# Staging the output weights of a hybrid decoder layer in seven idle buffers instead of one

## The chip, the cores and the metric

The kernel runs on one core of one Trainium2 chip. The metric is the device time of one execution in microseconds (us); a profile adds, for one execution, when each instruction ran on each engine (PE = TensorE, DVE = VectorE, ACT = ScalarE, POOL = GpSimd, SP = the queue that issues the DMAs).

## The reference, cut to what matters

One decoder layer over 2048 tokens of width 1024: an input projection feeds three head groups, their gated outputs are concatenated, mapped by one output matrix and normalised. The part around the change is the end:

```
cat = concat([o_att * silu(g_att), o_ssm * silu(g_ssm), o_mem * silu(g_mem)])   # (2048, 1024)
sub = cat @ w_out                                                               # (1024, 1024)
h   = layer_norm(DN_ALPHA * x + sub, ln_g, ln_b)
```

`o_att` is sparse attention (8 query heads, the keys of each query chosen by an indexer), `o_ssm` a state-space scan with a GLU, `o_mem` attention into 256 memory tokens.

## The kernel before, in words

Tokens are cut into 16 tiles of 128. In a first phase the input projection is made and the keys are chosen. In the second phase (`phase2`) the attention goes through (tile, head pair) items; tile 15, the longest, comes last. After the twelfth finished tile `stage_s5` runs the state-space group, and directly behind it `open_out` brings in the output weights. After the last attention tile, `out_prep` makes the operands of output tiles 0 and 1, and then `outputs` does all 16 output tiles.

Matmuls in full precision are made from rounded halves: a matrix is split in a high half (rounded copy) and a low half (the rest), and three products are added. So `open_out` makes two copies of `w_out`, `woh` and `wol`. It does so in eight slices of 128 x 1024 (one slice per 128 rows of `w_out`): a DMA brings the slice into a staging tile (L1217), ACT rounds it to `woh` (L1218), POOL subtracts to get `wol` (L1219). The staging tile is named `xh` and has one buffer, so the DMA of a slice waits until POOL is through with the slice before.

`out_prep` for a tile loads `cat` (three DMAs, L1226 to L1228) and the gates `aG` (three DMAs, L1230 to L1232), takes the tanh of the gates into `xh` on ACT (L1234), forms gate times (tanh + 1) on DVE (L1235) and multiplies into `cat` on POOL (L1236). PE transposes `cat` (L1243), ACT rounds to `ch` (L1244), DVE makes `cl` (L1245). For tiles 0 and 1 these tiles lie in the pool of `open_out`, with one buffer each of `xh`, `cat` and `aG` and two each of `ch` and `cl`; every one is 4 KB per partition. For the later tiles they lie in a pool that takes the place of the attention's memory. `out_mm` does 48 matmuls of 512 columns for a tile (L1260 to L1262), adds the residual on DVE (L1263) and normalises.

In the attention, PE makes logits into `pl` (L1116, L1117; two PSUM buffers), DVE adds the mask into `S` (L1118), ACT takes the exponential in place (L1123), PE transposes into `pt` (L1140), ACT rounds to `hi` (L1144), DVE makes `lo` (L1145), PE multiplies with V into `acc` (L1147, L1148). At the end of an item ACT copies `acc` to `oT` (L1153; one buffer), PE transposes (L1156), DVE scales (L1160) and SP stores to `OAD` (L1162).

The code gives a program order; what stands behind what in the queue of an engine is settled when the kernel is compiled, by a simulated timeline (`schedule_with_timeline_sim=True`), with waits put in where data or buffers need them. Each engine then works through its queue in order. The branch behind `fallback` is for inputs on which the key choice failed.

Of the kernel before, what the change touches and what calls it, by code (L numbers as in the profile page):

```python
# [10 lines left out]
F32 = mybir.dt.float32  # L11
F32R = mybir.dt.float32r
# [4 lines left out]
OP = mybir.AluOpType  # L17
# [5 lines left out]
D = 1024  # L23
NT = 16
KT = 8
# [62 lines left out]
class Layer:  # L88
# [1120 lines left out]
    def open_out(self, sp):  # L1209
        nc = self.nc  # L1210
        wo = (sp.tile([128, KT, D], F32R, name="woh"), sp.tile([128, KT, D], F32R, name="wol"))
        gb = sp.tile([128, 2, D], F32, name="gb")
        nc.sync.dma_start(out=gb[:, 0], in_=self.t["ln_g"][None, :].broadcast_to([128, D]))
        nc.sync.dma_start(out=gb[:, 1], in_=self.t["ln_b"][None, :].broadcast_to([128, D]))
        for i in range(KT):
            r = sp.tile([128, D], F32, name="xh", bufs=1)
            nc.sync.dma_start(out=r, in_=self.t["w_out"][:, i * D:(i + 1) * D])  # L1217
            nc.scalar.activation(wo[0][:, i], r, AF.Copy)  # L1218
            nc.gpsimd.tensor_tensor(wo[1][:, i], r, wo[0][:, i].bitcast(F32), op=OP.subtract)  # L1219
        return wo, gb  # L1220

    def out_prep(self, i, sp, nb=1, cb=2):
        nc = self.nc
        g = nc.gpsimd
        cat = sp.tile([128, D], F32, name="cat", bufs=nb)
        nc.sync.dma_start(out=cat[:, 0:512], in_=self.OAD[i])  # L1226
        nc.sync.dma_start(out=cat[:, 512:768], in_=self.OSD[i * 128:(i + 1) * 128])
        nc.sync.dma_start(out=cat[:, 768:1024], in_=self.OMD[i])  # L1228
        G = sp.tile([128, D], F32, name="aG", bufs=nb)
        nc.sync.dma_start(out=G[:, 0:512], in_=self.GAD[i])  # L1230
        nc.sync.dma_start(out=G[:, 512:768], in_=self.GSD[i])
        nc.sync.dma_start(out=G[:, 768:1024], in_=self.GMD[i])  # L1232
        th = sp.tile([128, D], F32, name="xh", tag="xh", bufs=nb)
        nc.scalar.activation(th, G, AF.Tanh, scale=0.5)  # L1234
        nc.vector.scalar_tensor_tensor(G, th, 1.0, G, op0=OP.add, op1=OP.mult)  # L1235
        g.tensor_tensor(cat, cat, G, op=OP.mult)  # L1236
        ch = sp.tile([128, KT, 128], F32R, name="ch", bufs=max(cb, nb))
        cl = sp.tile([128, KT, 128], F32R, name="cl", bufs=max(cb, nb))
        for a in range(2):
            pt = self.ps_a.tile([128, 4, 128], F32, name="pt", bufs=3)  # L1240
            for j in range(4):
                k = 4 * a + j
                nc.tensor.transpose(pt[:, j], cat[:, k * 128:(k + 1) * 128], self.ident)  # L1243
            nc.scalar.activation(ch[:, 4 * a:4 * a + 4], pt, AF.Copy, scale=0.5)  # L1244
            nc.vector.scalar_tensor_tensor(cl[:, 4 * a:4 * a + 4], pt, 0.5, ch[:, 4 * a:4 * a + 4].bitcast(F32),  # L1245
                                           op0=OP.mult, op1=OP.subtract)
        return ch, cl
# [31 lines left out]
    def outputs(self, tiles, wo, gb, sp, nb=1):  # L1279

        for i in tiles:
            if i not in self.cc:
                self.cc[i] = self.out_prep(i, sp, nb, 1)
            self.out_mm(i, self.cc.pop(i), wo, gb, sp, nb)
            for j in range(i + 1, min(i + 1 + AHEAD, NT) if nb > 1 else 0):
                if j not in self.cc:
                    self.cc[j] = self.out_prep(j, sp, nb, 1)

    def flag(self):

# [122 lines left out]
```

## Time and profile before

| | |
|---|---|
| time, median of 3 runs | 1452.05 us (1448.55 to 1458.51) |
| profiled execution, its own time | 1448.58 us |
| span of the profiled execution | 1446.8 us |
| PE busy | 1340.5 us (93%) |
| DVE busy | 1055.4 us (73%) |
| ACT busy | 876.8 us (61%) |
| POOL busy | 521.8 us (36%) |

The span is what the trace covers; 1.8 us of the execution's time lie outside it. Busy time of an engine is the sum over its instructions, and an average over stages that have different limits.

### The profile page before, as it was taken

The page shows a single profiled execution, that of the slowest core. Times are in us where ns is not written, and L with a number is a line of the kernel's source. Part 1 is how long each engine was busy: PE and PEld are TensorE (multiplying, and loading weights), DVE is VectorE, ACT ScalarE, POOL GpSimd, SP SyncE. Part 2 cuts the span into 40 slices and gives each one's busy share as a digit, 9 for nine tenths or more (in the row PEclk, how much of TensorE's full clock was granted, in tenths as well). Part 3 has the DMA queues.
Part 4 walks back from the last instruction along what each step waited for, and adds up shares of the span by engine and source line. Part 5 has one row for each costly group of instructions (what it writes and reads, how often), then busy time and mean ns, then how long its engine had stood idle before and what let it go on. Part 6 is the DMA issues. An engine that isn't in the chain of part 4 may idle for free.

```text
span 1446.8 us, 25157 instructions
## 1 busy us (share of the span) xinstructions
PE 1340.5 (93%) x8398; PEld 1182.1 (82%) x8398; DVE 1055.4 (73%) x2191; ACT 876.8 (61%) x1727; POOL 521.8 (36%) x1028
## 2 busy tenths in 40 slices
PE   7898899998869999999999999999999998699996
PEld 5687789997758988988798999987878987588885
DVE  4545786699676998855778889887887885365763
ACT  4576866775547745356788888876655776222221
POOL 1777544345991110041000000037873003344441
PEclk9899999999979999999999999999999999799999
DMA  9897355456536477742222111032221132565532
GB/s 346 269 314 252 133 176 183 146 186 223 188 95 209 161 240 259 229 147 92 88 66 86 53 47 42 14 104 75 45 58 31 41 113 79 176 203 175 189 102 75
DMA packets 128714, 206.58 MB, mean 143 GB/s; under 512 B 25088, under 2 KB 81792, under 8 KB 128320
## 3 DMA queue, kind: packets, MB, share of 16 engines
q1 hardware_dynamic: 128576, 204.89, 43.4%
q8 instruction: 68, 1.11, 0.3%
q14 instruction: 70, 0.57, 0.1%
HBM read 124.00 MB, written 77.10 MB: 139 GB/s over the span
## 4 chain that ended last, share of the span: by engine, by line
PE 63%; DVE 10%; POOL 9%; DMA 8%; issue 5%; ACT 5%; SPq 1%; POOLq 0%; ACTq 0%; DVEq 0%
PE fx L371 7%; PE fx L372 6%; PE fx L373 6%; PE pt L1140 6%; PE pl L1116 3%; PE pl L1117 3%; PE acc L1148 3%; PE acc L1147 3%; DVE sc L453 3%; PE pi L442 2%; PE pl L1260 2%; DMA xh<-w_out 2%; PE pl L1262 2%; PE pl L1261 2%; PE fx L1260 2%
## 5 line engine op out<-in xcount | busy, mean ns | idle before, releaser
L371 PE MATMUL fx<-whi,xhi 128*128 128x256 f32 (+3 forms) x912 | 306.1, 336 | 8.1 <-ACT xhi L139 3.6
L373 PE MATMUL fx<-whi,xlo 128*128 128x256 f32 (+3 forms) x912 | 304.8, 334 | 1.4 <-DMA xlo<-XD 1.4
L372 PE MATMUL fx<-wlo,xhi 128*128 128x256 f32 (+3 forms) x912 | 304.2, 334 | 0.0
L1145 DVE TENSOR_TENSOR lo<-pt,hi 128x512 fp32r<-128x512 f32 (+1 forms) x288 | 183.4, 656 | 50.3 <-ACT hi L1144 49.1
L453 DVE SCALAR_TENSOR_TENSOR sc<-rl,wsc,sc 128x1024 f32<-128x1024 f32 (+7 forms) x154 | 175.8, 1142 | 49.6 <-ACT rl L449 45.4
L371 PEld LDWEIGHTS fx<-whi,xhi 128*128 128x128 f32 x912 | 175.1, 192 | 26.1 <-ACT xhi L139 4.0
L1144 ACT ACTIVATE hi<-pt 128x512 fp32r<-128x512 f32 (+1 forms) x288 | 156.4, 578 | 58.8 <-PE pt L1140 28.8
L373 PEld LDWEIGHTS fx<-whi,xlo 128*128 128x128 f32 x912 | 174.6, 192 | 16.6 <-DMA xlo<-XD 1.9
L372 PEld LDWEIGHTS fx<-wlo,xhi 128*128 128x128 f32 x912 | 175.0, 192 | 15.1
L1123 ACT ACTIVATE S<-S,mx 128x1024 f32<-128x1024 f32 (+15 forms) x128 | 154.4, 1208 | 42.1 <-DVE mx L1118 39.8
L1140 PE MATMUL pt<-ident,S 128*128 128x128 f32 x1088 | 169.2, 276 | 10.0 <-ACT S L1123 5.3
L449 ACT ACTIVATE rl<-pi 128x1024 f32<-128x1024 f32 (+7 forms) x176 | 140.2, 816 | 58.1 <-PE pi L442 39.5
L1140 PEld LDWEIGHTS pt<-ident,S 128*128 128x128 f32 x1088 | 129.4, 144 | 22.5 <-ACT S L1123 8.1
L1148 PE MATMUL acc<-lo,V 128*128 128x256 f32 x544 | 143.5, 292 | 4.6 <-DVE lo L1145 4.6
L1147 PE MATMUL acc<-hi,V 128*128 128x256 f32 x544 | 143.5, 290 | 2.2 <-ACT hi L1144 1.9
L1118 DVE CUSTOM_DVE_ANT_0 S<-pl,mb,mx 128x512 f32<-128x512 f32 (+3 forms) x192 | 124.0, 646 | 19.6 <-PE pl L1117 15.2
L1116 PE MATMUL pl<-K,qs 128*128 128x512 f32 x320 | 133.1, 417 | 5.3 <-DVE mx L1118 4.9
L1117 PE MATMUL pl<-K,qs 128*128 128x512 f32 x320 | 117.2, 367 | 0.0
L1148 PEld LDWEIGHTS acc<-lo,V 128*128 128x128 f32 x544 | 102.5, 188 | 12.5 <-DVE lo L1145 8.8
L442 PE MATMUL pi<-kidx,qst 128*128 128x512 f32 (+3 forms) x304 | 95.2, 390 | 16.3 <-ACT rl L449 15.7
L1147 PEld LDWEIGHTS acc<-hi,V 128*128 128x128 f32 x544 | 102.5, 188 | 7.6 <-ACT hi L1144 2.8
L1118 DVE CUSTOM_DVE_ANT_0 S<-pl,mb 128x512 f32<-128x512 f32 (+3 forms) x128 | 80.9, 635 | 19.7 <-PE pl L1117 10.7
(350 smaller groups left out, 2891.6 us busy)
## 6 DMA issues: line engine op xcount, KB each, us to landing
xhi<-XD SPq DMA_DIRECT2D x32, 512.0 KB, 3.9
xlo<-XD SPq DMA_DIRECT2D x32, 512.0 KB, 5.0
QD<-kt SPq DMA_DIRECT2D x32, 256.0 KB, 2.3
qs<-QD SPq DMA_DIRECT2D x32, 256.0 KB, 3.0
xo<-x SPq DMA_DIRECT2D x16, 512.0 KB, 4.4
out<-xo SPq DMA_DIRECT2D x15, 512.0 KB, 2.7
raw<-xT SPq DMA_DIRECT2D x14, 512.0 KB, 5.3
XD<-xhi SPq DMA_DIRECT2D x14, 512.0 KB, 3.9
```

What stands on the lines that cost most here:

```text
L371: nc.tensor.matmul(p, x[0][:, k], w[0][:, k], start=(k == 0), stop=False)
L372: nc.tensor.matmul(p, x[0][:, k], w[1][:, k], start=False, stop=False)
L373: nc.tensor.matmul(p, x[1][:, k], w[0][:, k], start=False, stop=(k == KT - 1))
L453: nc.vector.scalar_tensor_tensor(dst, rl[:, :cw], wsc[:, h:h + 1], dst, op0=OP.mult, op1=OP.add, accum_out=stt[:, 0, ch:ch + 1] if h == 7 ...
L1116: nc.tensor.matmul(pl[:, :cw], qs[:, h], K[kh, g][:, kc:kc + cw], start=True, stop=False)
L1117: nc.tensor.matmul(pl[:, :cw], qs[:, h], K[kh, 2 + g][:, kc:kc + cw], start=False, stop=True)
L1118: nc.vector.tensor_tensor_reduce(S[:, c0:c0 + cw], pl[:, :cw], mb[:, c0:c0 + cw], scale=-0.125, scalar=(3e38 if ci == 0 else mx[:, ci - 1: ...
L1140: nc.tensor.transpose(pt[:, k, hj], P[hj][:, (k0 + k) * 128:(k0 + k + 1) * 128], self.ident)
L1144: nc.scalar.activation(hi[:, :kw], pf[:, :kw], AF.Copy)
L1145: nc.vector.tensor_tensor(lo[:, :kw], pf[:, :kw], hi[:, :kw].bitcast(F32), op=OP.subtract)
L1147: nc.tensor.matmul(acc[:, 0:256], V[(k0 + k) // 4][:, (k0 + k) % 4, g], hi[:, k], start=(k0 + k == 0), stop=False)
L1148: nc.tensor.matmul(acc[:, 0:256], V[(k0 + k) // 4][:, (k0 + k) % 4, g], lo[:, k], start=False, stop=(k0 + k == nk - 1))
```

## The change

Each of the eight slices gets a staging tile by a list of tags: slices 0 and 7 use the buffer of `xh`, slice 1 that of `cat`, slice 2 that of `aG`, slices 3 and 4 the two of `ch`, slices 5 and 6 the two of `cl`. These are the buffers in which `out_prep` later makes the operands of output tiles 0 and 1. The subtraction of the odd slices moves from POOL to DVE. The argument `cb` of `out_prep` goes; for the calls on the main path the number of buffers stays as it was.

```
-            r = sp.tile([128, D], F32, name="xh", bufs=1)
+            tag = ("xh", "cat", "aG", "ch", "ch", "cl", "cl", "xh")[i]
+            r = sp.tile([128, D], F32, name="wr", tag=tag, bufs=1 + (tag in ("ch", "cl")))
             nc.sync.dma_start(out=r, in_=self.t["w_out"][:, i * D:(i + 1) * D])
             nc.scalar.activation(wo[0][:, i], r, AF.Copy)
-            nc.gpsimd.tensor_tensor(wo[1][:, i], r, wo[0][:, i].bitcast(F32), op=OP.subtract)
+            (nc.vector if i % 2 else nc.gpsimd).tensor_tensor(wo[1][:, i], r, wo[0][:, i].bitcast(F32), op=OP.subtract)
...
-    def out_prep(self, i, sp, nb=1, cb=2):
+    def out_prep(self, i, sp, nb=1):
...
-        ch = sp.tile([128, KT, 128], F32R, name="ch", bufs=max(cb, nb))
-        cl = sp.tile([128, KT, 128], F32R, name="cl", bufs=max(cb, nb))
+        ch = sp.tile([128, KT, 128], F32R, name="ch", bufs=max(2, nb))
+        cl = sp.tile([128, KT, 128], F32R, name="cl", bufs=max(2, nb))
...
-                self.cc[i] = self.out_prep(i, sp, nb, 1)
+                self.cc[i] = self.out_prep(i, sp, nb)
```

## Rows read from the trace of the kernel before

**Rows 1.** The page's chain that ended last, by line, shares of the span.

```profile
PE fx L371 7%; PE fx L372 6%; PE fx L373 6%; PE pt L1140 6%; PE pl L1116 3%; PE pl L1117 3%; PE acc L1148 3%; PE acc L1147 3%; DVE sc L453 3%; PE pi L442 2%; PE pl L1260 2%; DMA xh<-w_out 2%; PE pl L1262 2%; PE pl L1261 2%; PE fx L1260 2%
```

**Rows 2.** The same chain in order of time: start us, duration us, what.

```profile
1202.53 3.48 DMA xh<-w_out
1206.04 1.07 ACT woh L1218
1207.17 2.40 POOL wol L1219
1209.59 3.75 DMA xh<-w_out
...
1231.18 3.87 DMA xh<-w_out
1235.09 1.08 issue
1236.21 2.35 POOL wol L1219
1238.58 1.06 ACT xh L1234
1239.67 1.24 DVE aG L1235
1241.03 2.35 POOL cat L1236
1243.42 1.97 PE pt L1243 x8
1245.39 0.63 PE pl L1260
...
1435.38 0.71 DVE xo L1263 x2
```

**Rows 3.** Busy time by stretch: length, PE, PEld, DVE, ACT, POOL, PEclk, DMA share, GB/s.

```profile
1176.00:1231.00 55.00, 45.21 (x307) 38.77 (x305) 35.90 (x82) 36.56 (x54) 16.47 (x7) 0.97 0.39 111
1231.00:1246.00 15.00, 2.58 (x10) 2.25 (x11) 1.92 (x2) 3.29 (x4) 4.83 (x3) 0.53 0.97 339
...
1260.00:1446.80 186.80, 175.53 (x832) 146.08 (x830) 110.07 (x138) 46.32 (x74) 78.39 (x76) 0.98 0.43 144
```

**Rows 4.** Waits from 1176 to 1246: us in total, times, longest us.

```profile
ACT woh L1218 <- DMA xh<-w_out: 15.1, 7, 6.1
...
PE pt L1140 <- ACT S L1123: 4.4, 2, 2.8
```

**Rows 5.** Groups by shape: ACT from 1176 to 1231, then POOL and DVE whole span.

```profile
L1218 ACT ACTIVATE woh<-xh 128x1024 fp32r<-128x1024 f32 x7 | 7.4, 1057 | 9.0 <-DMA xh<-w_out 9.0
...
L1219 POOL TENSOR_TENSOR wol<-xh,woh 128x1024 fp32r<-128x1024 f32 x8 | 19.0, 2370 | 120.6 <-DMA aG<-GSD 85.7 <-ACT woh L1218 34.9
...
L134 DVE TENSOR_TENSOR wlo<-raw,whi 128x1024 fp32r<-128x1024 f32 x4 | 5.0, 1262 | 0.0
```

**Rows 6.** DMA from 1175 to 1187: packets and rate; issues, KB each, us to landing.

```profile
DMA packets 1584, 2.95 MB, mean 246 GB/s; under 512 B 176, under 2 KB 816, under 8 KB 1584
...
xh<-w_out SPq DMA_DIRECT2D x1, 512.0 KB, 7.6
...
OAD<-oT SPq DMA_DIRECT2D x1, 64.0 KB, 6.2
```

**Rows 7.** Timeline, instructions of DVE and POOL that ran side by side.

```profile
1208.35 0.75 DVE L1118 CUSTOM_DVE_ANT_0 S<-pl,mb,mx 128x512 f32<-128x512 f32 x1 [0.99 <-PE pl L1117]
...
1263.66 2.39 POOL L1236 TENSOR_TENSOR cat<-cat,aG 128x1024 f32<-128x1024 f32 x1
1263.72 3.40 DVE L1276 SCALAR_TENSOR_TENSOR xo<-xo,lnst,gb 128x1024 f32<-128x1024 f32 x1 [0.47 <-POOL lnst L1271]
```

**Rows 8.** Timeline, SP's queue, ACT's `oT` and the last matmuls of the attention.

```profile
1176.45 0.47 SPq L1226 DMA_DIRECT2D cat<-OAD  x1
...
1192.27 0.37 ACT L1153 ACTIVATE oT<-acc 128x256 f32<-128x256 f32 x1
...
1229.06 0.66 PE L1156 MATMUL acc<-ident,oT 128*128 128x64 f32 x4 [1.08 <-ACT oT L1153]
```

More of the change, by code (lines that the diff above doesn't have):

```diff
@@ L1286, in outputs @@
                 if j not in self.cc:
-                    self.cc[j] = self.out_prep(j, sp, nb, 1)
+                    self.cc[j] = self.out_prep(j, sp, nb)
     def flag(self):
```

## The prediction

> **What bounds the kernel now.** I read the page's chain first. TensorE carries most of it, but one transfer stands among the matmuls with 2% of the span, the load of the output weights [rows 1]. So I followed the chain in order of time to where that load lies. There it runs round and round through one staging buffer: load 3.5 us, ScalarE 1.07, GpSimd 2.40, next load, a period of 7.06 us [rows 2]. The eighth slice is through at 1238.58. Only then is `xh` free for the tanh of output tile 0, and a chain of four engines follows before its first matmul at about 1245.2 [rows 2]. The attention's last matmuls are at 1229.06 to 1229.72 [rows 8]: TensorE is empty from there until the transposes at 1243.42.
>
> The table by stretches shows the price. From 1231 to 1246 TensorE works 2.58 of 15 us, at a mean granted clock of 0.53, little over the lower of its two levels (1.2 of 2.4 GHz), after it has stood still since 1229.72. From 1260 on it works 175.53 of 186.8 us, and what is missing is the tail after the last matmul (1435.38 to 1446.8) [rows 2, 3]. The output stage is therefore TensorE alone: it ends a fixed time after it starts. The question is when it can start.
>
> There is a second price, in the attention. From 1176 to 1231 TensorE works 45.21 of 55 us; without the 1.3 us after its last matmul, 8.5 us are lost [rows 3, 8]. The list of waits says why: ScalarE, which serves its queue in order, stood before a weight slice that had not landed for 15.1 us in seven waits, the longest 6.1 of them after the attention [rows 4]. The other six sum to 9.0 [rows 5], and the exponentials of the attention are queued behind them: TensorE waited 4.4 us for `S` in two of its waits [rows 4].
>
> **The change part by part, against the profiled execution's own 1448.58 us.** This execution is 3.5 us faster than the median of 1452.05; the sum is made on it and carried over to the median.
>
> Seven loads at once. The DMAs before them, 1.05 MB of `gb`, stay where they are; seven slices add 3.67 MB. The crowd after 1175 ran at 246 GB/s [rows 6], the one after 1231 at 339 [rows 3]: 19.2 or 13.9 us, so the seventh slice lands at 1194 or 1189. I take the slower end, because it is measured at that place. The eighth needs `xh`, which slice 0 frees after its landing at about 1183.5 (7.6 us after issue [rows 6]) plus 1.06 and 2.37 us; it lands a little behind the seventh, say at 1196. With ScalarE's 1.06 and VectorE's 1.26 [rows 5] the staging ends at 1198 to 1200 in place of 1238.58. These loads are ready at issue, and SP issues one in 0.47 us [rows 8], so a store of the attention behind them in SP's queue is held some 3 us; nobody waits for it before the next `oT` at 1192.27 [rows 8].
>
> The loads for output tile 0. Now they are issued at 1176.45, between the first and the second slice [rows 8], because their buffers are free. After the change these buffers hold slices 1 and 2 and come free at about 1190: later than now, but still before 1200. This row also shows that queue order is not program order: what is ready goes out ahead of what is earlier in the code. So I expect the preparation of tile 0 inside the attention: from 1200, and 4.84 us from tanh to transposes (1238.58 to 1243.42 [rows 2]), so at 1205, over 20 us before the attention ends. Tile 1 needs `cat` and `aG` again, and follows by about 1217. The cover is thus 12 us at the least.
>
> The attention. ScalarE's waits go in part: the first slice stays behind `gb`, and a slice of the crowd can still be late. At best all 8.5 us of lost TensorE time come back. Against it VectorE gets four subtractions of 1.26 us, 5.0 us (the same shape and types, L134 [rows 5]), and the two preparations, 2 x (1.24 + 2 x 0.75) = 5.5 us by L1235 [rows 2] and, for the two `cl` of a tile, by `S` of the same 128 x 512 from PSUM [rows 7]. VectorE is idle for 55 - 35.9 = 19.1 us there [rows 3], so 10.5 us find room, though not always at the right moment. ScalarE gets one more conversion and the tanh and `ch` of two tiles, some 5 us, and gives up about as much waiting. At worst the four subtractions take 3.40 us each, the next paragraph but one. I take 2 us earlier in all, near the row of the waits that are lost now (9.0) less what the new work may hold up.
>
> The start of the output stage. With the operands ready, what lies between the last attention matmuls and the first output matmul is at worst the transposes, 1.97 us at the low clock [rows 2]; at best nothing, if they slip into the attention. I take 1. With the `oT` transposes the first output matmul then comes at 1227.6: 17.6 us earlier than 1245.2. TensorE has no pause in which its clock falls: the 2.58 us that it worked at 0.53 [rows 3] would be 1.4 at full clock, so another 1.2 us. What becomes late next: tiles 2 to 4, whose buffers take the attention's place, are loaded from its end on; tiles 0 and 1 cover them with two times 11.8 us (a tile is 48 matmuls and 8 transposes; 832 instructions in 175.53 us [rows 3]), and a load in a crowd (7.6) with 6.6 us of chain is ready within 15. Nothing is charged. The renamed default of `out_prep` costs nothing on the main path, since the counts are the same there.
>
> Sum: 17.6 + 1.2 = 18.8 us. 1448.58 - 18.8 = 1429.8 for this execution; carried over to the median, 1452.05 - 18.8 = 1433.2, say 1433. If every idle us of TensorE between 1176 and 1246 went (9.8 + 12.4, and 1.2 for the clock), it would be 23.4, and 1428.7.
>
> **A rule against the change.** In the trace a VectorE instruction of the form of L1235 (1.24 us [rows 2]) took 3.40 us when it started 0.06 us behind a 2.39 us GpSimd instruction, both with two inputs in SBUF; the two durations nearly add up. `S` with one input in PSUM kept its 0.75 us beside the weight subtraction of GpSimd [rows 2, 7]. The Trainium skill states this as a rule ("SBUF — State Buffer", section "Who interferes with whom"): a VectorE instruction with two SBUF inputs and a GpSimd instruction that reads SBUF hold each other off, and the later one waits for the whole of the other. By that rule the new subtractions on VectorE cannot overlap those of GpSimd, and this trace agrees with it.
>
> **The rivals.** First, that hold-off. Subtractions of odd slices come while GpSimd works on even ones. At 3.40 us each they block VectorE for 13.6 us, and with 5.5 of preparation nothing is left of its 19.1 us. VectorE sets the pace then, and the excess of 4 x (3.40 - 1.26) = 8.6 us falls on the attention: 18.8 - 8.6 = 10.2 gained, 1441.9. For it speaks the row of 3.40; against it, that slices land nearly 2 us apart, so that the two engines alternate with short waits.
>
> Second, the change does only half of what it says: the tiles are staged early, but the preparation is queued behind the attention (its transposes share the three `pt` buffers). Then the chain of 6.6 us from tanh to first matmul [rows 2] stands behind 1226, at a fallen clock: first matmul at 1232.7, 12.5 us gained, 1439.5. For it speaks its place in the code; against it, row 1176.45.
>
> Third, slower: the crowd of loads starves the attention's own store. The store of an item takes 6.2 us in the small crowd [rows 6], `oT` has one buffer, and the next item writes it at 1192.27 [rows 8]. At 246 GB/s the 4.7 MB are through at 1194, a stall of 2 us. It eats the whole gain only if the store lands 19 us later, at 1211, that is if the crowd runs below 4.7 MB / 36 us = 130 GB/s; at 110 it would be 1218, and the time 7 us over now, 1459. No stretch with a crowd is so slow.
>
> **How the numbers follow.** A measurement of this kernel tells about 1% (14.5 us) from no change. Chances: my forecast 0.62 (gains from 14.5 to 24 us), the hold-off 0.16, the late preparation 0.15, the starved store 0.05, something else with no gain 0.02. Forecast plus the upper edge of the two middle rivals gives faster by over 1% 0.67; within 1% 0.28; slower 0.05. The range goes from 1425, the full recovery less a few us by which medians of three wander (they span 10 us here), to 1446, which takes in both middle rivals.
>
> **What would show it.** Seven weight loads issued within some 4 us of 1176, one more at about 1187; no GpSimd subtraction after 1200; tanh of tile 0 near 1200, not 1238; the first output matmul within 2 us of the last attention matmul, with no stretch at half clock; the attention's end at 1224 to 1230. VectorE subtractions of over 3 us would speak for the hold-off, a TensorE gap of 5 to 7 us before the output stage for the late preparation, waits for `OAD` at `oT` for the starved store. The forecast is wrong if ScalarE's waits in the crowd are as long as the 9.0 us now and the attention ends later than 1231, or if tile 2 comes late.

## The result, and the profile after

The changed kernel took 1434.72 us (median of 6 runs, 1432.55 to 1438.49) beside 1456.38 us for the kernel before in the same comparison (median of 6, 1448.55 to 1459.37): a ratio of 0.9861, 95% interval 0.9831 to 0.9890. Two repeats gave 0.9885 (0.9863 to 0.9907) and 0.9886 (0.9857 to 0.9916). The forecast was 1433, within 1425 to 1446. Three comparisons of the medians give a gain of 21.7, 15.8 and 18.2 us, where the forecast had 18.8, so the times alone size the gain only to some 3 us.

The profiled execution has a span of 1430.8 us, but two executions can't be laid on each other by their clocks: the first load of the output stage, the broadcast of `ln_g`, was issued at 1175.00 before and at 1177.51 after, by accidents upstream (two repeats of the changed kernel put it at 1181.39 and 1175.07). So every time below that is called "from the first load" is counted from that issue. The count is sound: in the profiles of all the kernels below, TensorE's work in the 30 us ahead of that issue is alike within 0.01 us for each 10 us, and the same number of attention matmuls (L1116, L1117, L1147, L1148) is left behind it. From it to the end of the span are 1446.8 - 1175.0 = 271.8 us before and 1430.8 - 1177.5 = 253.3 after: 18.5 us less, where the prediction's sum was 18.8.

The places that the counts of the kernel before rest on, from its timeline (start us, duration us, engine, line, operation):

```profile
1175.00 0.38 SPq L1213 DMA_DIRECT2D gb<-ln_g  x1
...
1227.70 0.28 PE L1148 MATMUL acc<-lo,V 128*128 128x256 f32 x1
...
1245.22 0.80 PE L1260 MATMUL pl<-woh,ch 128*128 128x512 f32 x1
```

The table of busy time by stretch, after the change (start and end us, length, PE, PEld, DVE, ACT, POOL with instructions, PEclk, DMA share, GB/s), answers to [rows 3]:

```profile
1176.00:1231.00 55.00, 47.54 (x327) 40.93 (x327) 47.41 (x95) 42.41 (x64) 13.08 (x5) 0.97 0.40 134
1231.00:1246.00 15.00, 15.00 (x75) 12.60 (x74) 3.77 (x9) 2.97 (x6) 2.81 (x3) 1.00 0.60 192
1246.00:1430.80 184.80, 173.70 (x824) 144.43 (x822) 109.41 (x137) 45.87 (x74) 77.63 (x76) 0.98 0.48 159
```

The second row is the gain: TensorE, which worked 2.58 us of this stretch at a granted clock of 0.53, now works all 15 at 1.00. The first row shows the price: VectorE goes from 35.90 to 47.41 us, ScalarE from 36.56 to 42.41.

SyncE's queue in the timeline, after (start us, duration us, queue, line, transfer, count), answers to the first row of [rows 8]:

```profile
1177.51 0.38 SPq L1213 DMA_DIRECT2D gb<-ln_g  x1
...
1178.45 4.58 SPq L1218 DMA_DIRECT2D wr<-w_out  x7
1184.67 0.33 SPq L1162 DMA_DIRECT2D OAD<-oT  x1
1189.52 0.33 SPq L1218 DMA_DIRECT2D wr<-w_out  x1
1192.37 0.33 SPq L1227 DMA_DIRECT2D cat<-OAD  x1
```

Seven loads go out at once, the eighth when slice 0 is through, and the loads of tile 0, which stood between the first and the second slice, 14.9 us from the first load (predicted 15).

The list of waits from 1176 to 1246, after (who waits, for whom: us in total, times, longest), answers to [rows 4]:

```profile
POOL cat L1237 <- DMA cat<-OMD: 25.6, 1, 25.6
...
ACT woh L1219 <- DMA wr<-w_out: 2.0, 1, 2.0
PE pt L1140 <- ACT S L1123: 2.0, 2, 1.4
ACT xh L1235 <- DMA aG<-GMD: 1.8, 1, 1.8
```

ScalarE's 15.1 us of waiting for weights in seven waits are 2.0 in one. No wait for the attention's store `OAD` appears: the starved store did not come about. The wait of 25.6 us is GpSimd's, for the second output tile, and is read below.

The timeline of the staging and of tile 0's preparation, after (start us, duration us, engine, line, operation, shapes, in brackets the idle time before and its releaser), answers to [rows 2]:

```profile
1185.97 1.06 ACT L1219 ACTIVATE woh<-wr 128x1024 fp32r<-128x1024 f32 x1 [2.01 <-DMA wr<-w_out]
...
1191.12 1.22 DVE L1220 TENSOR_TENSOR wol<-wr,woh 128x1024 fp32r<-128x1024 f32 x1
...
1196.80 5.71 POOL L1220 TENSOR_TENSOR wol<-wr,woh 128x1024 fp32r<-128x1024 f32 x2 [2.22 <-ACT woh L1219]
...
1197.81 2.47 DVE L1220 TENSOR_TENSOR wol<-wr,woh 128x1024 fp32r<-128x1024 f32 x1
1201.00 2.60 DVE L1220 TENSOR_TENSOR wol<-wr,woh 128x1024 fp32r<-128x1024 f32 x1
...
1203.93 1.06 ACT L1235 ACTIVATE xh<-aG 128x1024 f32<-128x1024 f32 x1
...
1206.43 2.38 POOL L1237 TENSOR_TENSOR cat<-cat,aG 128x1024 f32<-128x1024 f32 x1 [3.92 <-PE pt L1140]
...
1234.37 2.39 POOL L1237 TENSOR_TENSOR cat<-cat,aG 128x1024 f32<-128x1024 f32 x1 [25.56 <-DMA cat<-OMD]
```

The staging ends at 1203.6, 26.1 us from the first load instead of 63.6; the tanh of tile 0 comes 0.3 us later. The gated product of tile 0 is done at 1208.81, some 20 us before TensorE asks for it, that of tile 1 only at 1236.76.

TensorE at the change of stages, after, in the same view:

```profile
1229.23 0.60 PE L1244 MATMUL pt<-ident,cat 128*128 128x128 f32 x4
...
1230.14 0.60 PE L1244 MATMUL pt<-ident,cat 128*128 128x128 f32 x4
...
1230.70 0.40 PE L1261 MATMUL pl<-woh,ch 128*128 128x512 f32 x1
...
1231.17 0.28 PE L1148 MATMUL acc<-lo,V 128*128 128x256 f32 x1
...
1236.10 0.55 PE L1156 MATMUL acc<-ident,oT 128*128 128x64 f32 x4
...
1239.75 1.03 PE L1244 MATMUL pt<-ident,cat 128*128 128x128 f32 x8
```

No gap is left between the stages: the first output matmul (1230.70) runs before the attention's last ones (1231.17), and the attention's `oT` transposes (1236.10) stand amid the output's matmuls. From the first load the first output matmul comes at 53.2 us, before at 70.2.

### The profile page after: what moved, and what is told of

The parts are those of the page before. It is cut to its first block, busy times and chain, and to the rows that moved or that the text cites. A ratio compares the mean times of both kernels' runs of the same rounds, so it can differ in the third digit from the quotient of the medians.

```text
span 1430.8 us, 25169 instructions
## 1 busy us (share of the span) xinstructions
PE 1339.1 (94%) x8398; PEld 1181.4 (83%) x8398; DVE 1056.8 (74%) x2195; ACT 877.1 (61%) x1727; POOL 512.3 (36%) x1024
## 5 line engine op out<-in xcount | busy, mean ns | idle before, releaser
L453 DVE SCALAR_TENSOR_TENSOR sc<-rl,wsc,sc 128x1024 f32<-128x1024 f32 (+7 forms) x154 | 172.7, 1121 | 53.0 <-ACT rl L449 48.5
L1148 PE MATMUL acc<-lo,V 128*128 128x256 f32 x544 | 144.3, 293 | 3.3 <-DVE lo L1145 3.1
L1147 PE MATMUL acc<-hi,V 128*128 128x256 f32 x544 | 145.2, 293 | 1.8 <-ACT hi L1144 1.4
L1116 PE MATMUL pl<-K,qs 128*128 128x512 f32 x320 | 133.7, 419 | 8.7 <-DVE mx L1118 8.4
L1118 DVE CUSTOM_DVE_ANT_0 S<-pl,mb,mx 128x512 f32<-128x512 f32 (+3 forms) x192 | 123.8, 645 | 17.6 <-PE pl L1117 13.6
L1117 PE MATMUL pl<-K,qs 128*128 128x512 f32 x320 | 117.6, 368 | 0.0
L1148 PEld LDWEIGHTS acc<-lo,V 128*128 128x128 f32 x544 | 103.5, 190 | 11.3 <-DVE lo L1145 7.6
L1147 PEld LDWEIGHTS acc<-hi,V 128*128 128x128 f32 x544 | 103.6, 190 | 6.7 <-ACT hi L1144 2.1
```

Source lines behind the costliest of these rows:

```text
L453: nc.vector.scalar_tensor_tensor(dst, rl[:, :cw], wsc[:, h:h + 1], dst, op0=OP.mult, op1=OP.add, accum_out=stt[:, 0, ch:ch + 1] if h == 7 ...
L1118: nc.vector.tensor_tensor_reduce(S[:, c0:c0 + cw], pl[:, :cw], mb[:, c0:c0 + cw], scale=-0.125, scalar=(3e38 if ci == 0 else mx[:, ci - 1: ...
L1147: nc.tensor.matmul(acc[:, 0:256], V[(k0 + k) // 4][:, (k0 + k) % 4, g], hi[:, k], start=(k0 + k == 0), stop=False)
L1148: nc.tensor.matmul(acc[:, 0:256], V[(k0 + k) // 4][:, (k0 + k) % 4, g], lo[:, k], start=False, stop=(k0 + k == nk - 1))
```

## The experiments

**The theories.** That of the prediction: the gain is the end of the one-buffer chain, worth what TensorE stood still after the attention; which engine subtracts matters little as long as tile 0 is prepared before the attention ends. A rival that the prediction doesn't have: the gain, or much of it, comes from relieving GpSimd by VectorE. A further theory, formed on the trace after: of what the seven buffers give, a part is lost again to a crowd of staging work in the queues of ScalarE and VectorE, which the attention shares. Letters in the quoted expectations stand for the theories as each expectation puts them. All kernels leave the computation whole. The table gives what each came to; the last three columns are us from the first load in its profiled execution.

| kernel | ratio to before (95%) | last attention matmul starts | first output matmul | end of span |
|---|---|---|---|---|
| before | 1 | 52.7 | 70.2 | 271.8 |
| changed | 0.9861 (0.9831 to 0.9890) | 53.7 | 53.2 | 253.3 |
| changed, first repeat | 0.9885 (0.9863 to 0.9907) | 53.4 | 52.9 | 253.6 |
| changed, second repeat | 0.9886 (0.9857 to 0.9916) | 53.6 | 53.1 | 253.4 |
| seven buffers, subtractions on GpSimd | 0.9882 (0.9860 to 0.9903) | 53.3 | 52.9 | 254.7 |
| two buffers, subtractions on GpSimd | 0.9908 (0.9888 to 0.9929) | 56.0 | 56.2 | 257.1 |
| one buffer, odd subtractions on VectorE | 0.9983 (0.9969 to 0.9997) | 52.3 | 66.0 | 267.4 |
| preparation after the attention | 1.0086 (1.0054 to 1.0118) | 52.5 | 67.5 | 281.7 |
| seven buffers, subtractions on VectorE | 0.9915 (0.9891 to 0.9938) | 58.6 | 58.1 | 258.5 |
| constants loaded after the weights | 0.9893 (0.9871 to 0.9915) | 55.5 | 55.0 | 255.8 |
| all staging on GpSimd | 0.9943 (0.9926 to 0.9961) | 46.8 | 54.2 | 262.8 |
| roundings on GpSimd | 0.9867 (0.9836 to 0.9898) | 50.6 | 50.7 | 250.7 |
| roundings on GpSimd, again | 0.9863 (0.9842 to 0.9883) | 49.9 | 50.0 | 250.1 |
| odd roundings on GpSimd | 0.9877 (0.9844 to 0.9909) | 53.4 | 53.5 | 253.9 |

**The changed kernel again.**

> The changed kernel once more, as the measure for the others of this group: 0.986 of the kernel before, within 0.003. Both theories expect the same here.

It came to 0.9885, and the same places in the profile within 0.3 us. A second repeat stood beside the last kernels:

> The changed kernel once more on the same chip as the two with roundings on GpSimd, so that they can be compared with it directly: 0.984 to 0.990, first output matmul 52.5 to 53.5 us after the first issue.

It came to 0.9886.

**Only the buffers.** Seven buffers, every subtraction on GpSimd as before:

```
-            (nc.vector if i % 2 else nc.gpsimd).tensor_tensor(wo[1][:, i], r, ...)
+            nc.gpsimd.tensor_tensor(wo[1][:, i], r, ...)
```

> Seven staging buffers, but all eight subtractions on GpSimd. Theory A (the gain is the TensorE gap before the output stage, and it goes as soon as the staging ends some 8 us before the attention does): eight subtractions of 2.37 us from about 1187 us end at 1206 to 1208 instead of 1203.6, the tanh of tile 0 follows then, the transposes still come at the attention's end; ratio to the kernel before 0.984 to 0.988, no difference to the changed kernel, and VectorE's subtractions of 2.5 us are gone. Theory B (the halving of the subtraction work between two engines is a needed part): 4 to 6 us of the gain are lost, ratio 0.990 or more.

The whole gain, 0.9882, without VectorE's part: the staging ended at 29.4 us from the first load instead of 26.1, and ScalarE waited 0.5 us for it. By the profile 1.4 of the 18.5 us are missing (254.7 for 253.3). The rival by which VectorE's help makes the gain falls.

**Only VectorE.** One buffer as before, odd subtractions on VectorE:

```
-            tag = ("xh", "cat", "aG", "ch", "ch", "cl", "cl", "xh")[i]
+            tag = "xh"
```

> One staging buffer as before, but the odd slices subtracted on VectorE. Theory A: the chain of load, ScalarE and subtraction stays, four of its eight rounds are shorter by 2.37 - 1.25 = 1.1 us, so the output stage starts 4 to 5 us earlier: ratio 0.996 to 0.998, with the TensorE gap still near 10 us. Theory B: half the gain or more, ratio 0.993 or less.

The first output matmul came 4.2 us earlier than before, the end 4.4: four slices in the chain of one buffer at 1.23 instead of 2.37. The chain of waits still goes round from load to load, and the stretch between the stages is still there; its row by stretch (columns as above):

```profile
1230.00:1243.00 13.00, 2.60 (x10) 2.27 (x11) 3.44 (x4) 3.30 (x4) 2.34 (x1) 0.53 0.89 287
```

TensorE works 2.60 of 13 us at 0.53, as in [rows 3]. So the buffers make the gain.

**How many buffers.** Two, `xh` and `cat` in turn, all subtractions on GpSimd:

```
-            tag = ("xh", "cat", "aG", "ch", "ch", "cl", "cl", "xh")[i]
+            tag = ("xh", "cat")[i % 2]
```

> Two staging buffers in turn (those of xh and cat), all subtractions on GpSimd. Theory A: two slices per period of 7 to 8 us, so the staging ends at about 1212 to 1215, the chain of 5 us to the transposes ends before the attention's last matmuls near 1231: ratio 0.984 to 0.989, all of the gain with two buffers. Theory B (the gain goes with how fast the weights are in): the staging is 10 us later than with seven buffers, so the gain is about half, ratio 0.992 to 0.994.

Already two buffers give 271.8 - 257.1 = 14.7 of the 18.5 us in this one profile; the ratio, 0.9908, lies between the two expectations, and its interval overlaps those of the changed kernel. Their staging ends at 37.7 us, far ahead of the attention's end. Its attention ends 2.3 us later than the changed kernel's. ScalarE waits somewhat longer for weights, 4.8 us in four waits; the list of waits from 1171 to 1240 of this kernel:

```profile
ACT woh L1219 <- DMA wr<-w_out: 4.8, 4, 2.2
```

But TensorE's long stop comes later, and from another wait; its timeline:

```profile
1221.01 1.06 ACT L1235 ACTIVATE xh<-aG 128x1024 f32<-128x1024 f32 x1 [3.53 <-DMA aG<-GMD]
...
1222.60 0.39 PE L1147 MATMUL acc<-hi,V 128*128 128x256 f32 x1 [2.87 <-ACT hi L1144]
```

The tanh of output tile 1 stands in ScalarE's queue and waits 3.53 us for its gates, the attention's rounding to `hi` stands behind it, and TensorE stands still for 2.87 us, near the attention's end. That stop is longer than the 2.3 us.

**Where the preparation stands.** The changed kernel, but `out_prep` of tiles 0 and 1 only after the attention, staging untouched:

```
-            if i == NT - 1:
-                for j in range(2):
-                    self.cc[j] = self.out_prep(j, o[0])
```

> The changed kernel, but the operands of output tiles 0 and 1 are made with those of the others, in buffers that take the attention's place, so only after the attention. The staging stays as early as it is. Theory A (what counts is that the preparation of tile 0 gets in ahead of the attention's end): the loads of about 5 us and the chain of 6.6 us from tanh to first matmul stand behind the attention, so the first output matmul comes 64 to 67 us after the issue of the gb loads instead of 53, and 11 to 14 of the 18 us are lost: ratio to the kernel before 0.995 to 0.998. Theory C (early weights are what counts, the preparation is hidden anyway): as the changed kernel, 0.986 to 0.989.

Slower than before: 1.0086. The staging ended as early as in the changed kernel. Its timeline after the attention:

```profile
1234.51 0.28 PE L1148 MATMUL acc<-lo,V 128*128 128x256 f32 x1
...
1242.93 1.06 ACT L1235 ACTIVATE xh<-aG 128x1024 f32<-128x1024 f32 x1 [7.72 <-DMA aG<-GMD]
...
1247.77 1.97 PE L1244 MATMUL pt<-ident,cat 128*128 128x128 f32 x8 [11.85 <-POOL cat L1237]
...
1270.80 1.97 PE L1244 MATMUL pt<-ident,cat 128*128 128x128 f32 x8 [8.53 <-POOL cat L1237]
```

The first gap, 11.85 us, is the one expected. The second, 8.53 before the transposes of tile 1, was not: tile 1 is no longer ahead either, and these 8.5 us are two thirds of the 12.6 by which this output stage is longer than the one before (281.7 - 67.5 and 271.8 - 70.2). The first output matmul still comes 70.2 - 67.5 = 2.7 us earlier than before. This kernel gives up more than the change brought, though: in the kernel before the loads of tile 0 went out at 1176.45 [rows 8], here they come behind the attention, and ScalarE waits 7.72 us for the gates. So the run doesn't price early staging by itself; it shows that early staging is a loss when the next stage's loads and preparation come late.

**The other end of the split.** Seven buffers, every subtraction on VectorE:

```
-            (nc.vector if i % 2 else nc.gpsimd).tensor_tensor(wo[1][:, i], r, ...)
+            nc.vector.tensor_tensor(wo[1][:, i], r, ...)
```

> Seven staging buffers, all eight subtractions on VectorE, none on GpSimd. If the two engines hold each other off, none of the subtractions takes 2.5 us any more, all take 1.22 to 1.26. Theory A: VectorE has 8 x 1.22 = 9.8 us in the crowd instead of 7.5, the staging ends at the latest 2 us later than now, far ahead of the attention's end: ratio 0.985 to 0.989. Theory B (the halves on two engines are needed): 0.990 or more.

Groups by shape tell what a subtraction costs on each engine (count, busy us, mean ns of one). First the changed kernel, where they alternate:

```profile
L1220 POOL TENSOR_TENSOR wol<-wr,woh 128x1024 fp32r<-128x1024 f32 x4 | 10.7, 2679 | 86.4 <-DMA wr<-w_out 81.7 <-ACT woh L1219 4.7
...
L1220 DVE TENSOR_TENSOR wol<-wr,woh 128x1024 fp32r<-128x1024 f32 x4 | 7.5, 1878 | 0.0
```

Then the kernel with all on GpSimd, in the same view:

```profile
L1220 POOL TENSOR_TENSOR wol<-wr,woh 128x1024 fp32r<-128x1024 f32 x8 | 18.8, 2390 | 86.7 <-DMA wr<-w_out 85.6 <-ACT woh L1219 1.0
```

And the kernel with all on VectorE:

```profile
L1220 DVE TENSOR_TENSOR wol<-wr,woh 128x1024 fp32r<-128x1024 f32 x8 | 9.7, 1216 | 1.3 <-ACT woh L1219 1.3
```

Alone, one takes 1216 ns on VectorE and 2390 on GpSimd; side by side 1878 and 2679. The hold-off is real, and costs 4 x 0.66 = 2.6 us of VectorE. But the kernel without it is the slower one (1440.82 us by the median, for 1434.19 to 1436.21 of the changed kernel in its three comparisons), and 9.7 us of subtractions fall on VectorE in one go. Its busy time by stretch:

```profile
1190.00:1200.00 10.00, 6.02 (x33) 4.09 (x33) 9.85 (x19) 10.00 (x12) 0.00 (x0) 1.00 0.97 354
1200.00:1210.00 10.00, 7.89 (x29) 6.02 (x30) 8.98 (x15) 6.13 (x10) 0.79 (x1) 0.59 0.07 21
```

VectorE is busy for 9.85 of 10 us and ScalarE for 10.00. TensorE gets 6.02 us of work, and in the next stretch is granted 0.59, near the lower of its two levels, after it had stood still in part. The attention ends 4.9 us later than in the changed kernel, the span 5.2. In that second stretch ScalarE also stands still, before the tanh of tile 0, which needs the buffer of the last slice; an exponential of the attention is queued behind it. ScalarE's timeline:

```profile
1206.76 1.06 ACT L1235 ACTIVATE xh<-aG 128x1024 f32<-128x1024 f32 x1 [3.87 <-DVE wol L1220]
```

How the 4.9 us divide between VectorE's crowd, the clock and this wait isn't shown.

**An earlier first slice.** The 1 MB of broadcast constants behind the weights instead of ahead of them (the two lines of `gb` moved below the loop; "from the first load" is here the first weight load):

```
+        for i in range(KT):
+            ...
         nc.sync.dma_start(out=gb[:, 0], in_=self.t["ln_g"][None, :].broadcast_to([128, D]))
         nc.sync.dma_start(out=gb[:, 1], in_=self.t["ln_b"][None, :].broadcast_to([128, D]))
```

> The changed kernel with the two loads of gb (1.05 MB) issued after the eight weight slices instead of ahead of them. Theory A: the first slice lands some 3 us earlier after its issue, ScalarE's wait of 2.0 us for it goes, the staging ends about 3 us earlier, and nothing of that reaches the end, since the staging was 25 us early: ratio 0.985 to 0.989, first output matmul 51.5 to 53 us after the first of these loads. Theory B (the gain goes with how fast the weights are in): 3 us more gained, 0.984 or less.

No gain: 0.9893, the first output matmul at 55.0, later than expected. The staging ended at 22.8 us instead of 26.1, yet the attention ended later. ScalarE's timeline:

```profile
1216.78 1.06 ACT L1235 ACTIVATE xh<-aG 128x1024 f32<-128x1024 f32 x1 [2.96 <-DMA aG<-GMD]
```

The tanh of tile 1 holds ScalarE's queue for 2.96 us (1.76 in the changed kernel), and TensorE then waits 1.91 us for the attention's `oT` behind it, which is about what the attention's end lost (55.5 for 53.7).

**The crowd itself.** Rounding and subtraction all on GpSimd:

```
-            nc.scalar.activation(wo[0][:, i], r, AF.Copy)
-            (nc.vector if i % 2 else nc.gpsimd).tensor_tensor(wo[1][:, i], r, ...)
+            nc.gpsimd.tensor_copy(wo[0][:, i], r)
+            nc.gpsimd.tensor_tensor(wo[1][:, i], r, ...)
```

> Seven staging buffers, and GpSimd does the rounding too, so ScalarE gets none of the eight conversions (8.5 us between 1186 and 1202, where it was busy all the time and TensorE was not). The price of a rounding on GpSimd of this size is not in the traces: between 1.05 us (ScalarE's) and 2.4 (GpSimd's subtraction). The staging then ends 28 to 39 us after its first landing, 37 to 48 us after the gb loads, with the chain of 5 us before 53. Theory A with ScalarE as what holds the attention in the crowd: first output matmul at 50 to 52 us after the gb loads in place of 53, ratio 0.982 to 0.987. If the crowd on ScalarE costs nothing: 53, ratio as the changed kernel. If the rounding takes over 2.4 us the staging comes too late and the ratio is over 0.990.

Now the attention's last matmul starts at 46.8 us. The right comparison is the kernel with the late preparation (52.5), since here too no transposes stand inside: the staging on ScalarE and VectorE holds the attention up by 5.7 us. The price of a rounding turned out low (1.05 us), so none of the cases expected came about. Yet the kernel is slower than the changed one; its timeline:

```profile
1202.74 11.79 POOL L1220 TENSOR_TENSOR wol<-wr,woh 128x1024 fp32r<-128x1024 f32 x5
...
1225.61 0.28 PE L1148 MATMUL acc<-lo,V 128*128 128x256 f32 x1
...
1226.34 1.06 ACT L1235 ACTIVATE xh<-aG 128x1024 f32<-128x1024 f32 x1
...
1231.18 1.97 PE L1244 MATMUL pt<-ident,cat 128*128 128x128 f32 x8 [4.17 <-POOL cat L1237]
...
1251.59 1.97 PE L1244 MATMUL pt<-ident,cat 128*128 128x128 f32 x8 [5.99 <-POOL cat L1237]
```

The staging is done at 1214.53, and the last of tile 0's loads was issued at 1209.68, but ScalarE takes the tanh of tile 0 only after the attention: the prediction's second rival, with gaps of 4.17 and 5.99 us, in a kernel made for another question. So both halves are shown: the crowd costs 5.7 us, and a preparation that misses the attention costs more, since here the attention's last matmul starts 6.9 us earlier than in the changed kernel and the span ends 9.5 us later.

**Only the roundings off ScalarE.** The obvious mend: roundings on GpSimd, subtractions alternating as in the change.

```
-            nc.scalar.activation(wo[0][:, i], r, AF.Copy)
+            nc.gpsimd.tensor_copy(wo[0][:, i], r)
```

> The changed kernel with the rounding of all eight slices on GpSimd instead of ScalarE; the subtractions stay as they are, even slices on GpSimd, odd on VectorE. Worked from the runs so far (a rounding on GpSimd 1.04 us, a subtraction there about 2.4): GpSimd has 8 x 1.04 + 4 x 2.4 = 18 us, so the staging ends about 28 us after the issue of the first broadcast of the constants, and the ScalarE queue loses 8.5 us of work between the weights' arrival and the attention's end. Theory A (ScalarE's crowd delays the attention by 6 to 7 us, and the preparation of tile 0 stays ahead of its end): first output matmul 48 to 50 us after that issue (53 in the changed kernel), ratio to the kernel before 0.982 to 0.985. Theory B (the crowd on ScalarE costs nothing, the attention's own chain sets its end): as the changed kernel, 0.985 to 0.989. Theory C (the preparation falls behind the attention's end, as with all staging on GpSimd): a gap before the first output matmul, 0.990 or more.

The first output matmul came at 50.7, the end at 250.7, 2.6 us less than in the changed kernel: less than theory A expected, and the ratio, 0.9867, is not apart from the changed kernel's. Its timeline:

```profile
1200.11 5.70 POOL L1220 TENSOR_TENSOR wol<-wr,woh 128x1024 fp32r<-128x1024 f32 x2
...
1217.52 1.21 DVE L1220 TENSOR_TENSOR wol<-wr,woh 128x1024 fp32r<-128x1024 f32 x1
...
1218.77 1.06 ACT L1235 ACTIVATE xh<-aG 128x1024 f32<-128x1024 f32 x1 [0.76 <-DVE wol L1220]
...
1224.30 0.60 PE L1244 MATMUL pt<-ident,cat 128*128 128x128 f32 x4
...
1226.01 0.40 PE L1261 MATMUL pl<-woh,ch 128*128 128x512 f32 x1
```

GpSimd is through at 1205.81, but the last subtraction stands late in VectorE's queue, and the tanh that needs its buffer starts at 1218.77. Tile 0 is still ready before the attention ends, with little to spare. It was run once more, to see whether the 2.6 us are chance:

> The kernel with all roundings on GpSimd once more, since its first run (0.9867, profile 2.6 us shorter from the first broadcast of the constants to the end than the changed kernel) lies within the interval of the changed kernel. Theory A (the 2.6 us are real): first output matmul 50 to 51 us after the issue of the first broadcast, end about 251 us after it, ratio 0.984 to 0.988. Theory B (chance of one execution): first output matmul 52.5 to 53.5 us after it, end 253 to 254, ratio 0.986 to 0.989.

50.0 and 250.1: in two executions of this kernel the stretch is 250.1 and 250.7 us long, in three of the changed one 253.3 to 253.6. Some 3 us are shown in the profiles; the ratios alone, 0.9867 and 0.9863, don't tell the two kernels apart.

**Half of the roundings.** Odd slices rounded on GpSimd, even ones on ScalarE:

```
-            nc.scalar.activation(wo[0][:, i], r, AF.Copy)
+            self.round("gpsimd" if i % 2 else "scalar", wo[0][:, i], r)
```

> The changed kernel with the rounding of the odd slices on GpSimd, of the even ones on ScalarE. ScalarE loses 4.2 us, GpSimd has 4 x 1.04 + 4 x 2.4 = 13.8 us. Theory A: about half of the gain of the kernel with all roundings on GpSimd, first output matmul 50 to 52 us after the first issue, ratio 0.984 to 0.987. Theory B: as the changed kernel. Theory C: as the changed kernel or worse, with a wait for GpSimd's gated product ahead of the transposes of tile 0.

No gain over the changed kernel (53.5 and 253.9, 0.9877), where a half was expected: the effect of the crowd is not in proportion to the work moved.

## Why the prediction was right, and where it was not

The forecast's case came about: 18.5 us by the two profiles for a sum of 18.8. Of these, 70.2 - 53.2 = 17.0 stand before the first output matmul (predicted 17.6) and 1.5 behind it (predicted 1.2 for the clock, not charged for anything else). The kernels with one part of the change show the mechanism: buffers alone give all but 1.4 us of it, VectorE alone 4.4 us, and early staging without early loads and preparation a loss. That the sum came out within 0.3 us is in part luck, since three of its terms were off and cancel.

**The loads** were right: seven issued within 4.6 us, the eighth 12.0 us from the first load, as predicted (1187), tile 0's at 14.9. **The end of the staging**, predicted 23 to 25 us from the first load, came at 26.1; the gated product of tile 0 was still 20.4 us ahead of its transposes, so this cost nothing.

**The attention** was mis-sized. The step "I take 2 us earlier in all" measured 1.0 us later (53.7 for 52.7). The kernel with the late preparation splits it. With the staging alone the attention ends at 52.5, 0.2 us earlier: ScalarE's waits went, as said, but the eight roundings now come close together, and VectorE's subtractions with them, so that what one cause gave back the other took. The remaining 1.2 us up to 53.7 fit TensorE's own work that slipped in, two groups of transposes (0.60 us each) and the first output matmul; the wait of 1.8 us before tile 1's tanh in ScalarE's queue, which the late preparation doesn't have there, wasn't separated from it. The step set ScalarE's new work equal to the waiting that it gives up, and counted on a gain all the same. The crowd is shown by the kernel with all staging on GpSimd: its attention ended 5.7 us earlier than that of the late preparation.

**The start of the output stage** was mis-sized the other way. The 1227.6 comes out if one counts from the end of the attention's last L1148 before (1227.70 + 0.28 = 1227.98; the rows that it names show the `oT` transposes): 2 us earlier, "I take 1", and 0.66 for the `oT` transposes, so 1.66 us from that end to the first output matmul. After, the first output matmul starts 0.75 us ahead of that end (1230.70, and 1231.17 + 0.28 = 1231.45), since the output's first matmuls overlap the attention's last, and the `oT` transposes stand behind them. So one term lost 3.0 us, the other won 2.4, and 17.0 for 17.6 is luck.

**The clock** was charged at the wrong place. Of the 2.58 us that TensorE worked at 0.53, 1.97 are the transposes of tile 0 [rows 2], which lie ahead of the first output matmul, so most of the 1.2 us is already in the 17.6. What stood behind that matmul wasn't counted: the clock was still low when the output stage began. Its next stretch before (columns as in [rows 3]):

```profile
1246.00:1260.00 14.00, 13.75 (x59) 11.14 (x58) 4.09 (x8) 2.49 (x5) 2.82 (x3) 0.90 0.26 91
```

The clock is 0.90 here, and 1.00 in the changed kernel from 1231 to 1246. The first eight output matmuls before take 3.6 us (1245.22 to 1248.80), eight later ones 1.8 (1250.23 to 1252.05): 1.8 us, near the 1.5 that were measured. So 1.5 for 1.2 is luck too.

**The place of the preparation** was wrong without consequence. Transposes of tile 0 were expected at 30 us, right behind the gated product; they came at 51.7, behind attention work in TensorE's queue. As `cat` is free only after them, tile 1's loads into `cat` were held, GpSimd waited 25.6 us, and tile 1 was transposed 62.2 us from the first load (1239.75), not at 42. The matmuls of tile 0 cover that; the prediction had counted on that cover only for tiles 2 to 4. Why the order put the transposes there wasn't tried.

**The hold-off** came in between. Subtractions on VectorE were priced at 1.26 with 3.40 as the bound; two of four took 1.22 and two 2.47 and 2.60, 7.5 us in all for 5.0 and 13.6. The last one starts 1.51 us ahead of GpSimd's end (1201.00, and 1196.80 + 5.71 = 1202.51) and ends 1.09 us behind it (1203.60): it did its work almost wholly after GpSimd had finished. GpSimd paid as well, 5.71 us for two that take 2 x 2.39 alone. So what an overlap costs is what is left of the other engine's instruction; 3.40 was the price of a start at the same moment, and these two started later in it. The Trainium skill's rule ("SBUF — State Buffer", section "Who interferes with whom") lets the one that comes second wait until the other is through; the ends of these rows agree. The rival's price of 10.2 us gained was not seen, and without any such overlap (all subtractions on GpSimd) the ratio is within the intervals of the changed kernel.

## What to carry to other kernels

Where a staging loop runs through one buffer at the seam of two stages, read from the chain of waits what the period is and who stands still behind the last slice; two buffers gave 14.7 of the 18.5 us here by one profile, though the times don't tell them from seven. Staging early pays only if the next stage's first operands are loaded and prepared early too, so check where the scheduler puts that preparation. Check also what this preparation waits for: a tanh that waited for its gates or its buffer held the earlier stage's work behind it in ScalarE's queue (3.53 us with two buffers, 2.96 with the constants last, 3.87 with all subtractions on VectorE). That an engine is idle on average doesn't make work moved into an earlier stage free: look for stretches of 10 us in which it becomes 100% busy, and consider an engine that the stage leaves alone.

## What the runs showed of the hardware

GpSimd rounds a 128x1024 slice from f32 to fp32r in 1048 ns (mean of 8, kernel with all staging there), no slower than ScalarE's 1063, while the subtraction of the same shape takes it 2.39 us, twice VectorE's 1.22. So of the two steps the rounding is the one that GpSimd does at no loss when it is alone. Beside VectorE's subtractions it isn't: with roundings on GpSimd and odd subtractions on VectorE (first run) the roundings took 1167 ns on the mean, and the two subtractions that began while GpSimd rounded took 2.01 and 1.93 us, the other two 1.22 and 1.21.

The crowd of weight slices moved 354 GB/s with TensorE, VectorE and ScalarE at work and GpSimd idle (kernel with all subtractions on VectorE, 1190 to 1200), above the 246 that the prediction took from [rows 6] and the 339 of [rows 3]. Nothing followed from it: in the changed kernel ScalarE waited for weights only once, 2.0 us before the first slice, so its queue and not the transfers set the staging's pace.
